# A two-layer decoder trunk: order of the FFN output products, and how stick-breaking q and k are stacked

## The chip, the cores and the metric

One core of one Trainium2 chip runs the whole kernel in one launch. The metric is the device time of one execution in microseconds (us), the median of several runs.

## The reference

The input is one sequence of 512 tokens with 1024 features. There are two layers; each is a mixer between two half-step SwiGLU feed-forward networks (FFNs), so there are four FFNs in all. Layer 0 mixes with a hybrid block (a gated recurrence beside attention with a forget gate), layer 1 with stick-breaking attention over 16 heads of 64 features.

```python
def _swiglu(h, w_in, w_out):
    a, b = jnp.split(h @ w_in, 2, axis=-1)
    return (jax.nn.silu(a) * b) @ w_out

# stick-breaking attention, one block of 128 queries
z = jnp.einsum('bhqd,bhkd->bhqk', qi, k) * scale
log_nb = jnp.where(mask, jax.nn.log_sigmoid(-z), 0.0)
after = lax.cumsum(log_nb, axis=3, reverse=True) - log_nb
w = jnp.where(mask, jnp.exp(jax.nn.log_sigmoid(z) + after), 0.0)
return jnp.einsum('bhqk,bhkd->bhqd', w, v)

for layer in range(2):
    x = x + 0.5 * _swiglu(_rmsnorm(x, g0), w_in0, w_out0)
    x = x + mixer(_rmsnorm(x, gm))
    x = x + 0.5 * _swiglu(_rmsnorm(x, g1), w_in1, w_out1)
```

The hidden width of an FFN is 2816, that is 22 tiles of 128.

## The kernel before

Everything is stored transposed, features on the 128 partitions and the 512 tokens along the row. Each fp32 operand is split into a rounded part `hi` (a cast on ScalarE, ACT) and the rest `lo` (a subtraction on VectorE, DVE), and each product is made of three matmuls on TensorE (PE): hi by hi, hi by lo, lo by hi. `split` (line 116) loads a weight and splits it, `parts` (line 443) splits one that is loaded or computed. The pool `wp` holds these weights for the whole kernel: three buffers `raw`, four `hi`, four `lo`.

In an FFN (`ffn`, line 330) the hidden tiles j run in five chunks: 0 to 3, 4 to 7, 8 to 11, 12 to 15, 16 to 21. The tiles of the first chunk are plain products of 512 columns (`plain`). From the second chunk on two hidden tiles at a time (`pair`, line 466) are computed by Strassen's scheme of seven products in place of eight. A product (`product`, line 450) is 24 matmuls of 256 columns with a weight of its own, w1, w2, w5, w6, w3, w7, w4 in the order in which they are used; the weights other than w1, w2 and w4 are sums that DVE makes (`add`, line 460). The products accumulate in three PSUM banks, `px` (w1, w6, w7, w4), `py` (w2) and `pz` (w5, w3), and ACT and DVE read them between (`keep`, `plus`, line 488), before the next product adds to the same bank. The seventh product, of w4, is `tail`: it is handed to the next pair, which calls it as `before()` behind its own w1 product, so that on PE the order is w1, w4 of the pair before, w2, w5, w6, w3, w7. In the last pair of an FFN the tail follows behind the pair. The operands (`ops`, made by `g_inputs`) are prepared during the first pair, step by step, with `next(operands)`.

`outputs(c, done)` (line 534) multiplies the hidden tiles of a finished chunk by the output weights: eight units, one for each 128 output features, each of 12 matmuls of 512 columns for a chunk of four, and of 18 for the last chunk of six. One split weight serves two units (in the last chunk one). A unit ends with the addition to x on DVE (line 549). Its PSUM bank is the tag `mm` (three banks, shared with `px`) or `po` (one). The outputs of chunk c-1 are made while chunk c is computed: `between(i)` (line 573) takes whole units behind certain products of the pair, by the table `OUTPUTS` (line 48). The outputs of the last chunk run at the end, one behind the other.

PE executes in the order of the code (`manual_schedule`). The instructions of the other engines and of the DMA queue are ordered by a planner at compile time, which takes the ready one that stands first in the code; the queue on SyncE (SP) and each engine then run in that order.

In stick-breaking attention (`stick`, line 1066) heads go in pairs p = 0 to 7, two heads (e, o) on the 128 partitions. `qk_tile(p)` projects q and k of a pair with 24 matmuls of 512 columns each; `evac` (line 1084) takes the result from PSUM. For each head a tile `qks` is built that holds 64 partitions of one half and 64 of another: for q the hi part and the lo part, for k the hi part twice. Besides, `kl` holds k's lo part with zeros in the other 64 partitions (two sets, for even and odd pairs). `score` (line 1124) takes them as operands of two matmuls (lines 1129 and 1130). Each block of scores then goes through ACT, GpSimd and DVE, is transposed (line 646), split into `tt` (lines 649 and 650) and multiplied by v (line 664). The other products of the stage fill PE between these steps (`Fill`, lines 188 to 218), weighed by an amount of work that must be done before each step. `stack` (line 292), four DMAs on SP, is used in the hybrid stage to build its own `qks`.

Of the kernel before, what the change touches and what calls it, by code (L numbers as in the profile page):

```python
# [1 line left out]

# [8 lines left out]
F32 = mybir.dt.float32  # L11
F32R = mybir.dt.float32r
# [34 lines left out]

OUTPUTS = [((0, 1, 2, 1, 1), (1, 0, 1, 0, 1)), ((0, 0, 2, 0, 2), (1, 0, 1, 0, 2)), ((0, 0, 2, 0, 2), (1, 0, 1, 0, 2)),
           ((0, 0, 1, 0, 1), (1, 0, 1, 0, 1), (1, 0, 0, 0, 1))]
# [19 lines left out]
def kernel(ctx: ExitStack, tc: tile.TileContext, x, par, ffn_in, ffn_in2, ffn_out, ffn_out2,  # L69
# [56 lines left out]
    def mm3(pt, pairs, start=True, stop=True):  # L126

        n = len(pairs)
        for i, ((ah, al), (bh, bl)) in enumerate(pairs):
            T.matmul(out=pt, lhsT=ah, rhs=bh, start=(start and i == 0), stop=False)  # L130
            T.matmul(out=pt, lhsT=ah, rhs=bl, start=False, stop=False)  # L131
            T.matmul(out=pt, lhsT=al, rhs=bh, start=False, stop=(stop and i == n - 1))  # L132

# [166 lines left out]
    def run(g):  # L300
        for _ in g:
            pass
# [27 lines left out]
    def ffn(f, g_next, last=False):  # L330
# [3 lines left out]
        with ExitStack() as es:  # L334
# [115 lines left out]
            def product(pt, w, o, start):  # L450
                h, l = ops[o]
                for c in range(2):
                    po = pt[:, 256 * c:256 * c + 256]
                    for k in range(4):
                        wh, wl = cols(w, 4 * c + k)
                        for q, (a, b) in enumerate(((wh, h), (wh, l), (wl, h))):
                            T.matmul(out=po, lhsT=a, rhs=b[:, k], start=start and c + k + q == 0,  # L457
                                     stop=k == 3 and q == 2, skip_group_check=not (start and c == 0))

# [6 lines left out]
            def pair(j, between, operands, before):  # L466
# [34 lines left out]
                between(0)  # L501
# [4 lines left out]
                between(1)  # L506
# [6 lines left out]
                between(2)  # L513
# [5 lines left out]
                between(3)  # L519
# [4 lines left out]
                between(4)  # L524
# [10 lines left out]
            def outputs(c, done):  # L535

                j0, j1 = CHUNKS[c]
                n = j1 - j0
                for d in range(KT):
                    if n > 4:  # L540
                        w = split(ffn_out2[f, d], n * P, "wo")
                    elif d % 2 == 0:
                        w2 = split(ffn_out[f, c, d // 2], D, "wo")
                    ws = [cols(w, k) if n > 4 else cols(w2, d % 2 * 4 + k) for k in range(n)]
                    tok = [slice(0, S)] if not (last and done) or d < KT - 1 else [slice(0, S // 2), slice(S // 2, S)]
                    for t in tok:
                        po = pmm() if (d + t.start) % 2 else psum("po", 1)
                        mm3(po[:, t], [(ws[k], tuple(q[:, t] for q in hid[j0 + k])) for k in range(n)])
                        V.scalar_tensor_tensor(out=xT[d][:, t], in0=po[:, t], scalar=0.5, in1=xT[d][:, t],  # L549
                                               op0=ALU.mult, op1=ALU.add)  # L550
                        if last and done:
                            SY.dma_start(out=out[d][:, t], in_=xT[d][:, t])
                    if done and not last:
                        prep(d, g_next)
                    yield
# [12 lines left out]
            def tail():  # L568
                pass

            for c in range(1, len(CHUNKS)):
                if f == 0 and c == 3:
                    channel_consts(gp.tile([P, S], F32, tag="p5", bufs=1, name="t4"))
                g = outputs(c - 1, False)
                for j, counts in zip(range(*CHUNKS[c], 2), OUTPUTS[c - 1]):
                    def between(i):
                        for _ in range(counts[i]):
                            next(g)

                    tail = pair(j, between, operands, tail)  # L580
                if c == len(CHUNKS) - 1:
                    tail()
                run(g)
# [482 lines left out]
    def stick(g_next):  # L1066
        with ExitStack() as es:
# [15 lines left out]
            def qk_tile(p):  # L1083
                def evac(j):
                    def go(pt):
# [6 lines left out]
                        halves = [slice(0, HD), slice(HD, P)]  # L1092
                        st = [mp.tile([P, S], F32R, tag=f"qk{j}{c}", bufs=2, name="qks") for c in "eo"]
                        if j == 0:

                            for t, a, b in zip(st, halves, halves[::-1]):
                                A.copy(out=t[a], in_=pt[a])
                                V.tensor_tensor(out=t[b], in0=pt[a], in1=t[a].bitcast(F32), op=ALU.subtract)
                            qk[p, j] = st
                        else:  # L1100
# [3 lines left out]
                            for t, l, a, b in zip(st, klo[p % 2], halves, halves[::-1]):  # L1104
                                A.copy(out=t[a], in_=kt[a])
                                V.tensor_tensor(out=l[a], in0=kt[a], in1=t[a].bitcast(F32), op=ALU.subtract)
                                A.copy(out=t[b], in_=kt[a])
                            qk[p, j] = st
# [144 lines left out]
```

## Time and profile before

| | us |
|---|---|
| median of three runs | 1869.08 |
| lowest and highest | 1867.19, 1870.18 |
| the profiled execution | 1865.11 |
| its span | 1863.4 |
| PE busy in the span | 1836.0 (99%) |
| DVE busy | 1413.3 (76%) |
| ACT busy | 955.3 (51%) |

The span is the stretch that the profile shows; the execution is 1.7 us longer. The granted clock of PE was 1.00 throughout. The first FFN takes about the first 345 us, the hybrid block goes to 575, the second and third FFN to 915 and 1258, stick-breaking to 1515, the last FFN to the end.

A timeline row gives start and duration in us, the engine, the line of the code, the operation and the tiles (out<-in, buffer numbers left out). The durations of matmuls overlap, so the pitch is read from start to start. PEld is PE's loading of weights, SPq the issuing of DMAs on SyncE. A row of `s<-`, `mm<-` or `t<-` with line 457 is a gate product; lines 130 to 132 with `wo` are output products.

### The profile page before, as it was taken

To read this page: it belongs to the slowest core of one execution; us is meant where nothing else is said; L and a number is where in the kernel's file an instruction comes from. 1 tells how busy PE (TensorE), PEld (TensorE's weight loads), DVE (VectorE), ACT (ScalarE), POOL (GpSimd) and SP (SyncE) were. 2 spreads that over 40 slices of the span, in tenths; PEclk is the share of its full clock that TensorE was granted. 3 is DMA by queue.
4 is the path that set the end of the run, shared out by engine and by line. 5 is a ranking of instruction groups with operands and counts; after the bars stand their busy time and mean duration, and the time that the engine had idled before them with its cause. 6 is when DMAs were issued, how large, how long until landed. Compare 5 with 4: busy or idle time off the path is not lost.

```text
span 1863.4 us, 29383 instructions
## 1 busy us (share of the span) xinstructions
PE 1836.0 (99%) x11818; PEld 1664.1 (89%) x11818; DVE 1413.3 (76%) x1892; ACT 955.3 (51%) x1399; POOL 122.2 (7%) x266
## 2 busy tenths in 40 slices
PE   8999999998999999999999999999999999999999
PEld 6899999898888899999889999988888888999997
DVE  8867776688878877676597777765889978777773
ACT  5444444467755444444454444445777654444441
POOL 2000000111100000000000000001333400000000
PEclk9999999999999999999999999999999999999999
DMA  5332332353233333332323333232212123333322
GB/s 184 102 103 92 104 113 75 95 163 108 81 94 102 102 97 97 102 114 77 128 80 109 106 103 102 88 99 98 69 57 69 57 91 102 97 111 105 96 76 95
DMA packets 57304, 183.65 MB, mean 99 GB/s; under 512 B 8016, under 2 KB 9296, under 8 KB 57168
## 3 DMA queue, kind: packets, MB, share of 16 engines
q1 hardware_dynamic: 57168, 181.77, 30.6%
q8 instruction: 93, 1.52, 0.3%
q14 instruction: 43, 0.35, 0.1%
HBM read 172.31 MB, written 2.10 MB: 94 GB/s over the span
## 4 chain that ended last, share of the span: by engine, by line
PE 88%; DVE 6%; ACT 2%; issue 2%; POOL 1%; DMA 0%; SPq 0%; POOLq 0%; DVEq 0%; ACTq 0%
PE mm L457 22%; PE s L457 11%; PE mm L130 6%; PE mm L132 6%; PE mm L131 6%; PE t L457 5%; PE po L130 4%; PE po L132 4%; PE po L131 4%; PE mm L246 2%; PE mm L248 2%; PE mm L247 2%; PE mm L227 1%; PE mm L228 1%; PE mm L229 1%
## 5 line engine op out<-in xcount | busy, mean ns | idle before, releaser
L446 ACT CAST hi_w<-sum 128x1024 fp32r<-128x1024 f32 x144 | 150.8, 1050 | 191.9 <-PE s L457 52.1
L447 DVE TENSOR_TENSOR lo_w<-sum,hi_w 128x1024 fp32r<-128x1024 f32 x144 | 176.0, 1224 | 95.3 <-ACT hi_w L446 94.7
L122 ACT CAST hi_wo<-raw_wo 128x1024 fp32r<-128x1024 f32 (+1 forms) x96 | 94.1, 980 | 152.4 <-PE mm L131 64.2
L446 ACT CAST hi_w<-raw 128x1024 fp32r<-128x1024 f32 x72 | 75.8, 1052 | 129.9 <-PE s L457 70.7
L123 DVE TENSOR_TENSOR lo_wo<-raw_wo,hi_wo 128x1024 fp32r<-128x1024 f32 (+1 forms) x96 | 108.8, 1133 | 23.7 <-ACT hi_wo L122 23.7
L132 PE MATMUL po<-g,lo_wo 128*128 128x512 f32 x320 | 125.1, 391 | 1.3 <-DVE lo_wo L123 1.3
L130 PE MATMUL mm<-g,hi_wo 128*128 128x512 f32 (+1 forms) x324 | 125.8, 388 | 0.0
L130 PE MATMUL po<-g,hi_wo 128*128 128x512 f32 x320 | 125.6, 392 | 0.0
L132 PE MATMUL mm<-g,lo_wo 128*128 128x512 f32 (+1 forms) x324 | 125.5, 387 | 0.0
L131 PE MATMUL mm<-g,hi_wo 128*128 128x512 f32 (+1 forms) x324 | 125.5, 387 | 0.0
L131 PE MATMUL po<-g,hi_wo 128*128 128x512 f32 x320 | 125.2, 391 | 0.0
L122 ACT CAST hi_w<-raw_w 128x1024 fp32r<-128x1024 f32 (+2 forms) x75 | 77.9, 1040 | 85.3 <-PE mm L131 42.5
L123 DVE TENSOR_TENSOR lo_w<-raw_w,hi_w 128x1024 fp32r<-128x1024 f32 (+2 forms) x75 | 90.7, 1209 | 30.0 <-ACT hi_w L122 29.8
L549 DVE SCALAR_TENSOR_TENSOR x<-mm,x 128x512 f32<-128x512 f32 (+1 forms) x81 | 55.3, 683 | 49.8 <-PE mm L132 49.3
L246 PE MATMUL mm<-hi_w,xh 128*128 128x256 f32 (+1 forms) x312 | 90.8, 291 | 2.2 <-DVE q L897 2.2
L463 DVE TENSOR_TENSOR sum<-a,a 128x1024 f32<-128x1024 f32 x36 | 44.1, 1225 | 58.4 <-DMA a<-in_dram 58.4
L248 PE MATMUL mm<-hi_w,xl 128*128 128x256 f32 (+1 forms) x312 | 88.4, 283 | 0.0
L247 PE MATMUL mm<-lo_w,xh 128*128 128x256 f32 (+1 forms) x312 | 88.2, 283 | 0.0
L447 DVE TENSOR_TENSOR lo_w<-raw,hi_w 128x1024 fp32r<-128x1024 f32 x72 | 87.8, 1219 | 0.0
L549 DVE SCALAR_TENSOR_TENSOR x<-po,x 128x512 f32<-128x512 f32 x80 | 55.1, 689 | 39.5 <-PE po L132 39.5
L457 PE MATMUL s<-t4l,hi_w 128*128 128x256 f32 x288 | 81.6, 283 | 0.0
L457 PE MATMUL s<-t2l,hi_w 128*128 128x256 f32 x288 | 81.4, 283 | 0.0
(480 smaller groups left out, 6314.7 us busy)
## 6 DMA issues: line engine op xcount, KB each, us to landing
raw_w<-in_dram SPq DMA_DIRECT2D x72, 512.0 KB, 3.4
a<-in_dram SPq DMA_DIRECT2D x72, 512.0 KB, 3.5
raw<-in_dram SPq DMA_DIRECT2D x72, 512.0 KB, 3.5
raw_wo<-in_dram SPq DMA_DIRECT2D x64, 512.0 KB, 3.5
raw_wo<-in_dram SPq DMA_DIRECT2D x32, 384.0 KB, 3.0
raw_who<-in_dram SPq DMA_DIRECT2D x16, 512.0 KB, 3.3
qks<-hs SPq DMA_DIRECT2D x24, 128.0 KB, 2.5
x<-in_dram SPq DMA_DIRECT2D x8, 256.0 KB, 4.6
```

The lines of the kernel that those rows point to most:

```text
L122: A.copy(out=hi[:, :n], in_=raw[:, :n])
L123: V.tensor_tensor(out=lo[:, :n], in0=raw[:, :n], in1=hi[:, :n].bitcast(F32), op=ALU.subtract)
L130: T.matmul(out=pt, lhsT=ah, rhs=bh, start=(start and i == 0), stop=False)
L131: T.matmul(out=pt, lhsT=ah, rhs=bl, start=False, stop=False)
L132: T.matmul(out=pt, lhsT=al, rhs=bh, start=False, stop=(stop and i == n - 1))
L246: T.matmul(out=pt, lhsT=ah, rhs=bh, start=(k == 0), stop=False)
L247: T.matmul(out=pt, lhsT=ah, rhs=bl, start=False, stop=False)
L248: T.matmul(out=pt, lhsT=al, rhs=bh, start=False, stop=(k == KT - 1))
L446: A.copy(out=hi, in_=src)
L447: V.tensor_tensor(out=lo, in0=src, in1=hi.bitcast(F32), op=ALU.subtract)
L457: T.matmul(out=po, lhsT=a, rhs=b[:, k], start=start and c + k + q == 0, stop=k == 3 and q == 2, skip_group_check=not (start and c == 0))
L549: V.scalar_tensor_tensor(out=xT[d][:, t], in0=po[:, t], scalar=0.5, in1=xT[d][:, t], op0=ALU.mult, op1=ALU.add)
```

## The change

1. The table `OUTPUTS` and the calls of `between` go. A queue of output products is kept for the FFN, and `product` takes from it one 512-column matmul at a time, evenly among its 24 matmuls of 256 columns; `quota` says how many a product takes. The outputs of chunk c-1 begin three products later than chunk c does (`LAG`) and run over into the first products of the next chunk. 96 matmuls are spread over 14 products, in the last chunk 84 over 18; the last 12 run behind the last tail.
2. In stick-breaking, q and k are split over all 128 partitions, one cast and one subtraction each, and the stacked tiles are filled by DMA: four for q, four for k and two for k's lo part.

```diff
-OUTPUTS = [((0, 1, 2, 1, 1), (1, 0, 1, 0, 1)), ((0, 0, 2, 0, 2), (1, 0, 1, 0, 2)), ((0, 0, 2, 0, 2), (1, 0, 1, 0, 2)),
-           ((0, 0, 1, 0, 1), (1, 0, 1, 0, 1), (1, 0, 0, 0, 1))]
+LAG = 3
...
+    def mm3_each(pt, pairs, done):
+        n = len(pairs)
+        for i, ((ah, al), (bh, bl)) in enumerate(pairs):
+            for q, (a, b) in enumerate(((ah, bh), (ah, bl), (al, bh))):
+                T.matmul(out=pt, lhsT=a, rhs=b, start=i + q == 0, stop=i == n - 1 and q == 2)
+                if i == n - 1 and q == 2:
+                    done()
+                yield
...
             def product(pt, w, o, start):
                 h, l = ops[o]
+                more = quota.pop(0) if quota else 0
+                at = 0
...
+                            at += 1
+                            for _ in range(at * more // 24 - (at - 1) * more // 24):
+                                next(queue[0])
...
                     for t in tok:
                         po = pmm() if (d + t.start) % 2 else psum("po", 1)
-                        mm3(po[:, t], [(ws[k], tuple(q[:, t] for q in hid[j0 + k])) for k in range(n)])
...
+                        yield from mm3_each(po[:, t], [(ws[k], tuple(q[:, t] for q in hid[j0 + k]))
+                                                       for k in range(n)], landed)
                     if done and not last:
                         prep(d, g_next)
-                    yield
...
-                g = outputs(c - 1, False)
...
+                queue[0] = chain(queue[0], outputs(c - 1, False))
+                n = 7 * (CHUNKS[c][1] - CHUNKS[c][0]) // 2
+                end = n if c == len(CHUNKS) - 1 else n + LAG
+                total = 84 if c == len(CHUNKS) - 1 else 96
+                steps = end - LAG
+                each = [(i + 1) * total // steps - i * total // steps for i in range(steps)]
+                if not quota:
+                    quota.extend([0] * LAG)
+                quota.extend(each)
+                for j in range(*CHUNKS[c], 2):
+                    tail = pair(j, operands, tail)
+            tail()
+            run(queue[0])
             run(outputs(len(CHUNKS) - 1, True))
...
+                        h, l = (mp.tile([P, S], F32R, tag=f"qk{c}", bufs=2, name="hs") for c in "hl")
                         if j == 0:
-                            for t, a, b in zip(st, halves, halves[::-1]):
-                                A.copy(out=t[a], in_=pt[a])
-                                V.tensor_tensor(out=t[b], in0=pt[a], in1=t[a].bitcast(F32), op=ALU.subtract)
+                            A.copy(out=h, in_=pt)
+                            V.tensor_tensor(out=l, in0=pt, in1=h.bitcast(F32), op=ALU.subtract)
+                            stack(st, h, l)
                         else:
                             kt = wk("kt", 1)
                             V.tensor_tensor(out=kt, in0=pt, in1=rb, op=ALU.mult)
-                            for t, l, a, b in zip(st, klo[p % 2], halves, halves[::-1]):
-                                A.copy(out=t[a], in_=kt[a])
-                                V.tensor_tensor(out=l[a], in0=kt[a], in1=t[a].bitcast(F32), op=ALU.subtract)
-                                A.copy(out=t[b], in_=kt[a])
+                            A.copy(out=h, in_=kt)
+                            V.tensor_tensor(out=l, in0=kt, in1=h.bitcast(F32), op=ALU.subtract)
+                            stack(st, h, h)
+                            for t, a in zip(klo[p % 2], (slice(0, HD), slice(HD, P))):
+                                SY.dma_start(out=t[a].bitcast(F32), in_=l[a].bitcast(F32))
```

The removed `between(i)` stood behind each product of `pair`; the body of `landed`, passed to `mm3_each` as `done`, is the addition to x of line 549 and, in the last outputs, the store.

## Rows read from the trace of the kernel before

**Rows 1.** the page, part 1: busy us (share of the span) and instructions
```profile
PE 1836.0 (99%) x11818; PEld 1664.1 (89%) x11818; DVE 1413.3 (76%) x1892; ACT 955.3 (51%) x1399; POOL 122.2 (7%) x266
```

**Rows 2.** windows (PE, PEld, DVE, ACT, POOL busy): gate stretches, stick-breaking, a first pair
```profile
sum 824.91, PE 824.91 PEld 776.93 DVE 604.28 ACT 383.93 POOL 0.00; mean PE 206.23 PEld 194.23 DVE 151.07 ACT 95.98 POOL 0.00
...
1258.00:1515.00 257.00, 251.18 (x1498) 220.26 (x1497) 216.21 (x360) 175.66 (x336) 77.20 (x195) 1.00 0.21 71
...
941.00:985.00 44.00, 44.00 (x241) 38.19 (x241) 40.08 (x45) 21.32 (x25) 0.00 (x0) 1.00 0.29 96
```

**Rows 3.** timeline of PE (start us, us, engine line op); lines are left out
```profile
136.59 0.39 PE L130 MATMUL mm<-g,hi_wo 128*128 128x512 f32 x1
...
139.31 0.28 PE L457 MATMUL s<-t2h,hi_w 128*128 128x256 f32 x1
...
142.16 0.28 PE L457 MATMUL mm<-t6h,hi_w 128*128 128x256 f32 x1
```

**Rows 4.** timelines of PE and of its weight loads at a border
```profile
206.56 0.28 PE L457 MATMUL mm<-t6h,lo_w 128*128 128x256 f32 x1
206.68 0.40 PE L130 MATMUL po<-g,hi_wo 128*128 128x512 f32 x1
206.91 0.40 PE L131 MATMUL po<-g,hi_wo 128*128 128x512 f32 x1
...
206.68 0.19 PEld L131 LDWEIGHTS po<-g,hi_wo 128*128 128x128 f32 x1
```

**Rows 5.** timeline of ACT, gate stage; brackets hold idle time before and releaser
```profile
139.28 1.05 ACT L122 CAST hi_wo<-raw_wo 128x1024 fp32r<-128x1024 f32 x1 [3.83 <-PE mm L131]
142.25 1.05 ACT L446 CAST hi_w<-raw 128x1024 fp32r<-128x1024 f32 x1 [1.91 <-PE s L457]
```

**Rows 6.** timeline of the DMA issues on SP, same stretch
```profile
132.14 0.33 SPq L440 DMA_DIRECT2D raw<-in_dram  x1
```

**Rows 7.** timelines of DVE and PE, first pair of the first FFN
```profile
68.36 1.24 DVE L123 TENSOR_TENSOR lo_wo<-raw_wo,hi_wo 128x1024 fp32r<-128x1024 f32 x1
...
69.65 0.50 PE L132 MATMUL po<-g,lo_wo 128*128 128x512 f32 x1 [1.29 <-DVE lo_wo L123]
```

**Rows 8.** timelines of PE and DVE, last pair of the first FFN
```profile
319.15 0.40 PE L130 MATMUL po<-g,hi_wo 128*128 128x512 f32 x1
...
321.90 0.28 PE L457 MATMUL mm<-t3h,hi_w 128*128 128x256 f32 x1
...
319.34 0.69 DVE L488 TENSOR_TENSOR ab<-mm,keep 128x512 f32<-128x512 f32 x1 [0.53 <-PE mm L457]
```

**Rows 9.** groups by line, stick-breaking stage (count, busy us, mean ns, idle before)
```profile
L1098 DVE TENSOR_TENSOR qks<-mm,qks 64x512 fp32r<-64x512 f32 x16 | 11.0, 688 | 1.1 <-ACT qks L1097 0.6
L1105 ACT CAST qks<-kt 64x512 fp32r<-64x512 f32 x16 | 9.9, 618 | 1.3 <-DVE kt L1103 1.2
L1097 ACT CAST qks<-mm 64x512 fp32r<-64x512 f32 x16 | 9.3, 581 | 6.9 <-DVE qks L1098 6.9
```

**Rows 10.** waits, stick-breaking stage (us in total, times, longest us)
```profile
ACT qks L1097 <- DVE qks L1098: 6.9, 7, 1.6
PE po L664 <- DVE tt L650: 4.1, 4, 1.3
```

**Rows 11.** timeline of SP, hybrid stage; DMA issues (KB each, us to landing)
```profile
521.08 0.59 SPq L296 DMA_DIRECT2D qks<-hs  x1
...
qks<-hs SPq DMA_DIRECT2D x24, 128.0 KB, 2.5
```

**Rows 12.** timelines of DVE and PE, pair 6 of the heads
```profile
1437.89 0.67 DVE L1103 TENSOR_TENSOR kt<-mm,rb 128x512 f32<-128x512 f32 x1
...
1442.68 0.28 PE L1130 MATMUL s<-kl0e,qks 128*128 128x128 f32 x1
```

**Rows 13.** timeline of weight loads, stick-breaking stage
```profile
1451.07 0.19 PEld L1129 LDWEIGHTS s<-qks 128*128 128x128 f32 x1
1451.18 0.19 PEld L1130 LDWEIGHTS s<-kl0e,qks 128*128 128x128 f32 x1
```

More of the change, by code (lines that the diff above doesn't have):

```diff
@@ L1 @@
 from contextlib import ExitStack
+from itertools import chain
 import numpy as np
@@ L464, in add, with pair @@
                 return t
-            def pair(j, between, operands, before):
+            def pair(j, operands, before):
                 src = ffn_in2[f, (j - PLAIN) // 2]
@@ L500, in pair @@
                 product(py, w2, 1, True)
-                between(0)
                 s2 = add(s1, a11, ALU.subtract, s1)
@@ L505, in pair @@
                 product(pz, w5, 4, True)
-                between(1)
                 p5 = keep(pz, gp, "p5")
@@ L512, in pair @@
                 product(px, w6, 5, False)
-                between(2)
                 u2 = keep(px, state, "acc")
@@ L518, in pair @@
                 product(pz, w3, 2, False)
-                between(3)
                 plus(quarter(0, 1), pz, u2)
@@ L523, in pair @@
                 product(px, w7, 6, False)
-                between(4)
                 plus(quarter(1, 1), px, p5)
@@ L547, in outputs, with landed @@
                         po = pmm() if (d + t.start) % 2 else psum("po", 1)
-                        mm3(po[:, t], [(ws[k], tuple(q[:, t] for q in hid[j0 + k])) for k in range(n)])
[L549 to L552, printed above, removed]
+                        def landed(po=po, d=d, t=t):
+                            V.scalar_tensor_tensor(out=xT[d][:, t], in0=po[:, t], scalar=0.5, in1=xT[d][:, t],
+                                                   op0=ALU.mult, op1=ALU.add)
+                            if last and done:
+                                SY.dma_start(out=out[d][:, t], in_=xT[d][:, t])
+                        yield from mm3_each(po[:, t], [(ws[k], tuple(q[:, t] for q in hid[j0 + k]))
+                                                       for k in range(n)], landed)
                     if done and not last:
                         prep(d, g_next)
-                    yield
+            queue = [iter(())]
+            quota = []
             es.enter_context(tc.manual_schedule(engines={mybir.EngineType.PE}))
@@ L573, in ffn @@
                     channel_consts(gp.tile([P, S], F32, tag="p5", bufs=1, name="t4"))
-                g = outputs(c - 1, False)
[L575 to L583, printed above, removed]
+                queue[0] = chain(queue[0], outputs(c - 1, False))
[11 more added lines that the diff above has]
+            run(queue[0])
             run(outputs(len(CHUNKS) - 1, True))
@@ L1091, in go @@
                                                 op0=ALU.mult)
-                        halves = [slice(0, HD), slice(HD, P)]
                         st = [mp.tile([P, S], F32R, tag=f"qk{j}{c}", bufs=2, name="qks") for c in "eo"]
+                        h, l = (mp.tile([P, S], F32R, tag=f"qk{c}", bufs=2, name="hs") for c in "hl")
+                        qk[p, j] = st
                         if j == 0:
-                            for t, a, b in zip(st, halves, halves[::-1]):
-                                A.copy(out=t[a], in_=pt[a])
-                                V.tensor_tensor(out=t[b], in0=pt[a], in1=t[a].bitcast(F32), op=ALU.subtract)
-                            qk[p, j] = st
+                            A.copy(out=h, in_=pt)
+                            V.tensor_tensor(out=l, in0=pt, in1=h.bitcast(F32), op=ALU.subtract)
+                            stack(st, h, l)
                         else:
@@ L1103, in go @@
                             V.tensor_tensor(out=kt, in0=pt, in1=rb, op=ALU.mult)
-                            for t, l, a, b in zip(st, klo[p % 2], halves, halves[::-1]):
-                                A.copy(out=t[a], in_=kt[a])
-                                V.tensor_tensor(out=l[a], in0=kt[a], in1=t[a].bitcast(F32), op=ALU.subtract)
-                                A.copy(out=t[b], in_=kt[a])
-                            qk[p, j] = st
+                            A.copy(out=h, in_=kt)
[3 more added lines that the diff above has]
+                                SY.dma_start(out=t[a].bitcast(F32), in_=l[a].bitcast(F32))
                     return go
```

## The prediction

> **What bounds the kernel now.** I read the page first. TensorE (PE) is busy 1836.0 of 1863.4 us [rows 1], so time is won or lost only where PE waits or where its matmuls stand further apart or closer. The windows by stage come next [rows 2]: in one long stretch from the gate stage of each of the four FFNs, 824.91 us together, PE is busy all 824.91, DVE 604.28 (73%) and ACT 383.93 (47%). In the stick-breaking stage PE is busy 251.18 of 257.00 us. So the FFN part of the change can't gain by removing waits, since these stretches have none; it gains only if matmuls come closer together. The stick part has 5.8 us of waits to work on.
>
> Third, the timeline of PE gives the pitch, start to start. 24 products of 256 columns take from 139.31 to 142.16, 0.119 us each; 12 of 512 columns take from 136.59 to 139.31, 0.227 each, and the first ones behind a gate product 0.23 [rows 3, 4]. At the border the 512 starts 0.12 us after the 256, as another 256 would, and the next 512 another 0.23 later [rows 4]: the pitch is set by a product's own width, not by its neighbour's.
>
> Fourth, the timeline of ACT shows how weights get their room. `hi` and `lo` have four buffers each, and a conversion (cast into `hi` on ACT, subtraction into `lo` on DVE) starts when PE gives one back. The casts keep the order of the code: a raw gate weight was fetched at 132.14, yet at 139.28 the returned buffer went to the output weight `hi_wo`, which stands earlier in the code, and the gate weight waited for the next one, at 142.25 [rows 5, 6]. That `hi_wo` is first used two gate products later, and this lead is why PE does not wait for it now.
>
> **The change part by part.**
> (1) Spreading. No matmul is added or removed. Of the 1536 output products that ran in units of 12, 4 x (3 x 96 + 84) = 1488 now stand singly, 6 or 7 (4 or 5 in the last chunk) in a run of 24 gate products. By the border rows that is worth nothing: a single 512 may take the 0.227 of a unit's end or the 0.23 of its start, and the units of now hold both [rows 3, 4]. Bounds 1488 x -0.003 to 1488 x +0.002, so -4.5 to +3; I take 0, between them.
>
> (2) The room for output weights. Today an output weight holds its buffer for one or two units. Spread out, its 24 matmuls last 3.5 products, and the next output weight is due at once after it: one of the four buffers is always taken. `split` still stands right ahead of the first matmul that uses it. I followed the four buffers in the order of the code, as [rows 5] show it. In chunks 1 to 3 the switch from one output weight to the next falls in two places: in the middle of w1's product (after 4 of its 7 single products) and at the start of w6's, each once a pair. When w1's product starts, the four hold w1, w4 of the pair before, w2 (next in the code) and the old output weight, so the new one must wait for the old one's buffer. `hi` of the old one is free after its 23rd matmul; from there to the first matmul with the new one lie 7 gate products and one output product, 7 x 0.119 + 0.23 = 1.06 us. The cast starts 0.09 us after PE's release (142.16, 142.25) and takes 1.05 us [rows 3, 5]; PE starts 0.06 us after its operand (68.36 + 1.24 = 69.60, 69.65), and that matmul stays 0.10 us longer, 0.50 where others have 0.40 [rows 4, 7]. That makes 1.30 against 1.06, a stall of 0.24 us. `lo` takes 1.24 us more [rows 7], ready at about 2.5; the third matmul is due at 1.06 + 2 x (0.23 + 3.5 x 0.119) + 0.24 = 2.6, so nothing is added if DVE is free. With DVE at 73% and ACT at 47% a conversion often sits out part of another instruction of 0.6 to 1.2 us. Bounds 0.2 and 1.5 us a switch; I take 0.5, nearer to the free case, since the code's order puts these conversions ahead of most others. 6 such switches an FFN, 24 in all: +12 us (5 to 36).
> At the switches in w6's product the buffers of w2 and w5 come back first. The source of w3 needs w6's subtraction and a DVE addition, so the output weight probably takes w2's buffer two products ahead and nobody waits; if not, it costs as above. Bounds 0 and 24 x 0.5 = 12 us; I take 0. In the last chunk only the switch in w1 of the third pair is short of time: 0 to 1 us, four times; I take +2.
>
> (3) The last tail. `tail` adds w4's product into `px`, whose content DVE must have read by then (line 488). In all pairs but the last, w1's product of the next pair lies between. In the last pair a unit of 12 lies there now, 319.15 to 321.90, and DVE reads in it from 319.34 for 0.69 us [rows 8]. After the change only one single product of 0.23 us covers it: 0.19 + 0.69 + 0.06 + 0.10 - 0.23 = 0.8 us, up to 2 if DVE is behind another instruction. I take 0.9 x 4 = +3.6 (3 to 8).
>
> (4) The first pair of each FFN. DVE prepares the operands there and is busy 40.08 of 44 us [rows 2]. Today 5 units (60 matmuls, some 13.7 us) stand in that pair and give it time, afterwards 20 (4.6 us). Against that, a `lo_wo` for which PE waits 1.29 us now [rows 7] is due later, behind 12 gate products. In the order of the code I find w3 and w7 ready ahead of their products, with little to spare. Bounds -1.3 and +8; I take 0.
>
> (5) Stick-breaking. For q two ACT casts of 0.58 and two DVE subtractions of 0.69 on 64 partitions become one of each on 128; for k four casts of 0.62 become one, two subtractions one [rows 9]. Eight pairs: 8 x (0.58 + 3 x 0.62) = 19.5 us of ACT and 8 x 2 x 0.69 = 11 us of DVE go, off PE's path except where PE waits. There the view of waits shows PE waiting for DVE's `tt` (line 650) 4 times, 4.1 us together, and ACT's second q cast waiting for the first subtraction 7 times, 6.9 us [rows 10]. I take 3 of the 4.1 as gone (bounds 0 and the stage's 5.8 us of idle).
> Added: 4 DMAs for q and 6 for k, 80 in all, on SP. In the hybrid stage such a DMA holds SP 0.59 us and lands 2.5 us after its issue [rows 11]. Behind them on SP stand the loads of raw weights; 10 x 0.59 = 5.9 us in a pair of some 26 us leaves them room, and they have three buffers of lead: 0. But k itself comes later: multiplication 0.67, cast 0.62, four issues 2.4, landing of the fifth 2.5 make 6.2 us, and in pair 6 its first score stands 1442.68 - 1437.89 = 4.8 us behind the multiplication [rows 12]: +1.4 us there (with the first and the last pair, which are near the limit too, 0 to 5); I take 1. Net of (5): -2 (-6 to +5).
>
> Sum: 0 + 12 + 0 + 2 + 3.6 + 0 - 2 = +15.6 us. The profiled execution took 1865.11 us, 1.7 beyond its span; the median of the three runs is 1869.08, 4.0 above it. The difference carries over: 1869.1 + 15.6 is about **1884.5 us**. 0.2% (3.7 us) is about what can be told from no change.
>
> **Rivals.**
> A. The output weights are converted early after all: the order on ACT is laid out anew, and they step ahead of w2, which has two products of time. Then (3) and (5) are left: 3.6 - 4 gives 1869, between 1864 and 1872. For it: gate weights have long leads. Against it: the casts keep the code's order where both sources are there [rows 5, 6].
> B. Weight loads were what spaces the 256-column products, and a single 512 gives them slack. In the gate stage a load starts with the matmul before its own [rows 4]; in the stick stage two loads follow each other after 0.11 us [rows 13]. If the 0.119 were the load's, one 256 for each 512 would fall to 0.11, 1488 x 0.008 = 12 us, and the 512s to 0.227, 4.5 us: 1869 - 16.5 = 1853 without the waits of (2) and (3), 1868 with them. Against it: the 256 right ahead of a 512 keeps 0.12 and the 512 its 0.23 [rows 4].
> [...]
> C. Slower by far: at every switch, w1's and w6's, the new conversion stands behind one more instruction on ACT and on DVE, some 1.1 us. It decides if DVE is near full around w1's product, where both gates, s1, w5 and w2 fall. 48 x (0.24 + 1.1) = 64 us and (3): 1937. Against it: DVE idles a quarter of the gate stage [rows 2].
>
> **How the numbers follow.** Forecast 0.52 (its own range 1873 to 1905, from the bounds of (2) to (5)), A 0.20, B 0.14, C 0.14. The range 1857 to 1908 holds A, two thirds of B and little of C: together about 0.8. Faster by over 0.2% (below 1865.3): most of B, a third of A and a little for a larger gain in (5), 0.21. Within 0.2%: the rest of A and B and the low end of the forecast, 0.20. Slower: 0.59.
>
> **What the profile would show.** Right: in the gate stages PE is no longer busy throughout, and rows of PE's output products name ACT `hi_wo` or DVE `lo_wo` as releaser, about 6 times an FFN, 0.2 to 1.5 us each; casts of `hi_wo` start in the middle of w1's product; PE waits for line 488 once near the end of each FFN; 0.119 and 0.23 stay. In the stick stage the four waits for `tt` are fewer, and PE waits before the first score of pair 6. Wrong: no such waits (A), or 256-column products beside a 512 at 0.11 (B).

## The result and the profile after

The changed kernel takes 1924.15 us (median of four runs, 1918.78 to 1925.38) against 1868.13 us for the kernel before: 1.0299 times as long, 95% interval 1.0284 to 1.0314, so 56 us slower (the median before is now of four runs, the three of the table in front and one more). The prediction was 1884.5 us with a range of 1857 to 1908. The profiled execution took 1918.78 us, 53.7 more than that of before (1865.11).

The page of the changed kernel, part 1, answers to [rows 1]. PE has the same number of instructions and is busy longer; DVE and ACT have 16 and 32 instructions less.

```profile
PE 1869.5 (98%) x11818; PEld 1676.3 (87%) x11818; DVE 1397.6 (73%) x1876; ACT 935.0 (49%) x1367; POOL 121.1 (6%) x266
```

Windows from the first to the last gate product of each FFN (us, then PE, PEld, DVE, ACT and POOL busy, the granted clock, DMA share, GB/s), first the sum line of the kernel before, then the four lines and the sum of the changed one:

```profile
sum 1056.98, PE 1055.69 PEld 993.39 DVE 777.89 ACT 483.43 POOL 0.00; mean PE 263.92 PEld 248.35 DVE 194.47 ACT 120.86 POOL 0.00
```
```profile
58.39:338.72 280.33, 272.46 (x1884) 251.29 (x1883) 197.13 (x230) 123.42 (x156) 0.00 (x0) 0.99 0.29 94
636.79:914.85 278.06, 272.62 (x1884) 251.32 (x1882) 191.33 (x209) 119.40 (x149) 0.00 (x0) 0.99 0.30 95
996.42:1273.71 277.29, 270.98 (x1884) 249.94 (x1882) 191.44 (x209) 119.35 (x149) 0.00 (x0) 1.00 0.30 95
1601.35:1877.74 276.39, 271.14 (x1883) 250.00 (x1882) 191.35 (x209) 119.43 (x149) 0.00 (x0) 1.00 0.30 95
sum 1112.07, PE 1087.21 PEld 1002.55 DVE 771.24 ACT 481.61 POOL 0.00; mean PE 271.80 PEld 250.64 DVE 192.81 ACT 120.40 POOL 0.00
```

All of the loss is here: 1112.1 - 1057.0 = 55.1 us. The stretch between the third and the fourth FFN's gate products, which holds stick-breaking, went from 330.1 to 327.6. PE's busy time shows only half of the loss (1112.07 - 1087.21 = 24.9 us not busy), because a matmul's recorded length (0.28 or 0.40 us) is more than its distance to the next (0.12 or 0.23), so a short wait is hidden under it, and matmuls at a slower pace count as busy as well. The starts tell more. I took the differences between starts of neighbouring matmuls in these stretches, called more than 15 ns over the usual 229 (512 columns) or 119 ns (256) a wait, and added these up by their place:

| place in the changed kernel | times | waits, us | predicted |
|---|---|---|---|
| w6's product of the first pair | 4 | 6.4 + 4.2 + 2.7 + 2.7 = 16.0 | 0 (-1.3 to +8) |
| w1's products | 24 | 22.2 | 12 (5 to 36) |
| w6's products of later pairs | 20 | 6.9 | 0 (0 to 12) |
| last chunk, w1's product of the third pair and others | 8 | 4.8 | 2 (0 to 4) |
| the last tail | 4 | 3.5 | 3.6 (3 to 8) |

The waits of PE and of its weight loads for output weights, and two of the stick stage (us in total, times, longest us), from the changed kernel:

```profile
PE po L138 <- ACT hi_wo L121: 12.0, 5, 3.8
PE po L138 <- DVE lo_wo L122: 3.3, 4, 0.8
PE mm L469 <- ACT hi_wo L121: 2.6, 4, 0.6
...
PE s L1150 <- DMA kl0e<-hs: 1.8, 1, 1.8
PE s L1150 <- DMA kl1e<-hs: 0.8, 1, 0.8
...
PEld po L138 <- ACT hi_wo L121: 25.2, 48, 4.0
PEld po L138 <- DVE lo_wo L122: 10.2, 27, 1.0
```

48 loads wait for `hi_wo` and 27 for `lo_wo`; before, PE's one wait for an output weight was that for `lo_wo` in [rows 7]. The four of `mm` on line 469 for `hi_wo` are misnamed: they are the last tails, whose gate product needs no output weight; what it waits for is DVE's line 503 (line 488 before).

**The first pair.** Timelines of PE, ACT and DVE in the third FFN of the changed kernel (start us, us, engine, line, operation; in brackets the idle time before and what ended it):

```profile
1005.27 0.28 PE L469 MATMUL mm<-t5h,hi_w 128*128 128x256 f32 x1
1007.96 0.50 PE L138 MATMUL po<-g,hi_wo 128*128 128x512 f32 x1 [2.42 <-ACT hi_wo L121]
...
1005.12 0.59 ACT L499 COPY keep<-s 128x512 f32<-128x512 f32 x1 [3.21 <-PE s L469]
1005.92 1.04 ACT L455 CAST hi_w<-sum 128x1024 fp32r<-128x1024 f32 x1 [0.21 <-DVE sum L478]
1006.87 1.04 ACT L121 CAST hi_wo<-raw_wo 128x1024 fp32r<-128x1024 f32 x1
...
1004.67 1.22 DVE L478 TENSOR_TENSOR sum<-raw,sum 128x1024 f32<-128x1024 f32 x1
```

ACT idles 3.21 us, then keeps p5, casts w3 as soon as DVE has made its source s4 (1004.67 + 1.22 = 1005.89), and only then casts `hi_wo`. In the code `hi_wo` stands behind w3's `parts`, as its `split` is called inside w6's product. Its raw weight had landed at 986.70. PE, which now meets its first output matmul four matmuls into w6's product, waits from 1005.39 (1005.27 + 0.12) to 1007.96.

**What the wait does to the clock.** Windows of the changed kernel, second FFN, where PE waits in the same place:

```profile
640.00:645.70 5.70, 5.70 (x51) 5.70 (x49) 4.28 (x6) 2.17 (x4) 0.00 (x0) 1.00 0.27 92
645.70:648.40 2.70, 0.28 (x3) 0.08 (x2) 1.59 (x2) 2.49 (x4) 0.00 (x0) 1.00 0.42 109
648.40:650.00 1.60, 1.60 (x8) 1.46 (x9) 1.60 (x3) 0.84 (x1) 0.00 (x0) 0.67 0.36 143
650.00:652.00 2.00, 2.00 (x10) 1.90 (x10) 0.87 (x1) 0.00 (x0) 0.00 (x0) 0.50 0.64 170
652.00:654.00 2.00, 2.00 (x15) 1.82 (x14) 0.00 (x0) 0.37 (x1) 0.00 (x0) 0.91 0.26 100
...
1008.00:1012.00 4.00, 4.00 (x28) 3.74 (x29) 2.50 (x3) 1.11 (x2) 0.00 (x0) 1.00 0.53 184
```

PE was busy throughout, then 0.28 of 2.70 us; after that the granted clock is at half, 0.50 from 648.95 to 652.37, and comes back to 1.00. That costs 1.5 us (4.2 in the table against 2.7), and as much in the first FFN, where it is 0.50 from 72.10 to 75.52, behind a wait of 4.0 us; behind the same wait of 2.6 us in the third (the last row) and fourth FFN the clock stayed at 1.00. The other three executions of the changed kernel have a mean granted clock of 0.993 to 0.995 where the profiled one has 0.997, and are 4.5 to 6.6 us longer. So the same wait of 2.6 us brings the loss in one FFN and not in two others, and the rows do not show why.

**The switches.** The second pair of a chunk, w1's product in the third FFN of the changed kernel (PE, ACT, DVE):

```profile
1055.40 0.39 PE L138 MATMUL mm<-g,lo_wo 128*128 128x512 f32 x1
...
1055.99 0.28 PE L469 MATMUL mm<-t0h,lo_w 128*128 128x256 f32 x1
1056.35 0.50 PE L138 MATMUL po<-g,hi_wo 128*128 128x512 f32 x1
1056.68 0.28 PE L469 MATMUL mm<-t0h,hi_w 128*128 128x256 f32 x1
...
1055.24 1.05 ACT L121 CAST hi_wo<-raw_wo 128x1024 fp32r<-128x1024 f32 x1 [0.87 <-PE mm L138]
...
1055.37 0.68 DVE L369 TENSOR_TENSOR g<-ab,g 128x512 fp32r<-128x512 f32 x1
1055.97 0.68 DVE L560 SCALAR_TENSOR_TENSOR x<-mm,x 128x512 f32<-128x512 f32 x1
1056.57 1.22 DVE L122 TENSOR_TENSOR lo_wo<-raw_wo,hi_wo 128x1024 fp32r<-128x1024 f32 x1
```

The cast starts when the old weight's `hi` comes back, and PE's matmul, due at 1055.99 + 0.12 = 1056.11, starts at 1056.35: 0.24 us late, as worked out in the prediction. It then holds PE 0.33 instead of 0.23. `lo_wo` stands behind the gate's subtraction and the addition of the unit just finished (line 560), ends at 1057.79, and costs the third matmul another 0.22 + 0.11. So a switch costs 0.67, where 0.5 was taken.

A switch in w6's product, the pair before (ACT; w2's product ends at 1034.90, w6's starts at 1039.36):

```profile
1035.01 1.05 ACT L455 CAST hi_w<-sum 128x1024 fp32r<-128x1024 f32 x1 [0.57 <-DVE sum L478]
...
1038.97 1.05 ACT L121 CAST hi_wo<-raw_wo 128x1024 fp32r<-128x1024 f32 x1 [2.90 <-PE mm L138]
```

The first is w3's cast, which runs as soon as w2's product is over. `hi_wo` waits 2.90 us for an output matmul (line 138), so it gets the old output weight's buffer here too, and PE stands 0.24 + 0.11 us at the switch.

### The profile page after: what moved, and what is told of

Same layout as the page of the kernel before. It is cut to its first block, busy times and chain, and to the rows that moved or that the text cites. A ratio compares the mean times of both kernels' runs of the same rounds, so it can differ in the third digit from the quotient of the medians.

```text
span 1917.1 us, 29573 instructions
## 1 busy us (share of the span) xinstructions
PE 1869.5 (98%) x11818; PEld 1676.3 (87%) x11818; DVE 1397.6 (73%) x1876; ACT 935.0 (49%) x1367; POOL 121.1 (6%) x266
## 5 line engine op out<-in xcount | busy, mean ns | idle before, releaser
L138 PE MATMUL mm<-g,hi_wo 128*128 128x512 f32 (+1 forms) x648 | 239.2, 391 | 0.0
L138 PEld LDWEIGHTS po<-g,hi_wo 128*128 128x128 f32 x640 | 120.7, 189 | 30.3 <-ACT hi_wo L121 25.2
L138 PE MATMUL po<-g,lo_wo 128*128 128x512 f32 x320 | 129.1, 404 | 4.7 <-DVE lo_wo L122 3.3
L138 PEld LDWEIGHTS mm<-g,hi_wo 128*128 128x128 f32 x648 | 121.6, 188 | 5.9
L560 DVE SCALAR_TENSOR_TENSOR x<-po,x 128x512 f32<-128x512 f32 x80 | 55.1, 689 | 90.5 <-PE po L138 90.5
L456 DVE TENSOR_TENSOR lo_w<-a,hi_w 128x1024 fp32r<-128x1024 f32 x36 | 44.1, 1225 | 68.6 <-ACT hi_w L455 68.6
L469 PE MATMUL mm<-t0h,lo_w 128*128 128x256 f32 x288 | 82.7, 287 | 1.8 <-DVE lo_w L456 1.7
L469 PE MATMUL mm<-t3h,hi_w 128*128 128x256 f32 x288 | 81.0, 281 | 2.6 <-ACT hi_wo L121 2.6
```

The source lines that it names most:

```text
L138: T.matmul(out=pt, lhsT=a, rhs=b, start=i + q == 0, stop=i == n - 1 and q == 2)
L456: V.tensor_tensor(out=lo, in0=src, in1=hi.bitcast(F32), op=ALU.subtract)
```

## The experiments

The kernel before took 1866.1 to 1866.6 us beside these runs; the ratios are to it. Stage times are from the starts in each profiled execution.

| run | us | ratio (95%) | gate stages, us | between FFN 3 and 4, us |
|---|---|---|---|---|
| kernel before | 1868.1 | 1 | 1057.0 | 330.1 |
| changed kernel | 1924.2 | 1.0299 (1.0284 to 1.0314) | 1112.1 | 327.6 |
| e1_stick_only | 1864.4 | 0.9985 (0.9976 to 0.9994) | 1057.3 | 326.8 |
| e2_ffn_only | 1927.1 | 1.0325 (1.0311 to 1.0339) | 1117.1 | 330.4 |
| e3_own_room | 1904.8 | 1.0198 (1.0181 to 1.0215) | 1098.0 | 327.1 |
| e4_early | 1878.9 | 1.0065 (1.0051 to 1.0079) | 1071.8 | 327.1 |
| e5_first_pair | 1906.9 | 1.0217 (1.0201 to 1.0232) | 1100.1 | 327.2 |
| e6_tail_cover | 1874.4 | 1.0041 (1.0028 to 1.0055) | 1068.6 | 326.7 |
| e7_threes | 1880.2 | 1.0072 (1.0058 to 1.0086) | 1071.8 | 327.6 |
| e8_by_head | 1861.4 | 0.9970 (0.9959 to 0.9982) | 1057.4 | 325.8 |
| e9_q_only | 1863.4 | 0.9989 (0.9981 to 0.9998) | 1057.2 | 327.2 |
| e10_twelves | 1872.1 | 1.0030 (1.0018 to 1.0042) | 1066.2 | 326.8 |

**One part at a time.** e1 has the FFN of before and the new `evac` of stick-breaking; e2 the new FFN and the old `evac`.

> The kernel before with the stick-breaking part of the change alone. Theory: the whole loss is in the FFN, and the stick stage gains what the trace of after shows between the gate stages of the third and the fourth FFN, 330.09 to 327.64 us: about 2.4 us below the kernel before (1864 to 1867). Rival: the gain of that stage came from the work that the spread FFN leaves at its borders, not from the stacking: then no difference, or slower by up to 3 us because PE waits before the first scores of pairs 6 and 7 (2.1 and 0.9 us in the trace of after). Each theory expects those two waits here as well.

> The changed kernel with the stick-breaking code of before: spreading alone. Theory: the two parts add up, so this is the changed kernel plus 2.4 us, about 1926 (58 us over the kernel before). Rival: the FFNs behind and ahead of the stick stage absorb part of it: below 1922.

2.0 us faster and 60.8 us slower: as the theory has it, the whole loss is the spreading and the stacking is a small gain. The two add up to 58.8, the changed kernel has 56.0; its lowest and highest run are 6.6 apart, so they are equal within what these runs tell. The waits before the first scores are in e1 too:

```profile
PE s L1130 <- DMA kl0e<-hs: 1.5, 1, 1.5
PE t L646 <- DVE be L1141: 0.6, 1, 0.6
PE po L664 <- DVE tt L650: 0.4, 2, 0.2
PE s L1130 <- DMA kl1e<-hs: 0.4, 1, 0.4
```

The waits of PE for `tt` fell from 4.1 us [rows 10] to 0.4, and ACT's wait for the first subtraction of q is no longer there.

**Room or order.** e3 gives every second output weight buffers of its own, e4 keeps four and changes only where the conversion stands in the code.

```diff
 # e3
-                        w2 = split(ffn_out[f, c, d // 2], D, "wo")
+                        w2 = split(ffn_out[f, c, d // 2], D, "wo", gp if d % 4 else None)   # own hi, lo in gp
```
```diff
 # e4; `early` is where outputs() looks before it splits, `sent` counts output matmuls
+            def ahead():
+                n = -(-sent[0] // 24)
+                if n < 16 and quota and 24 * n < sent[0] + quota[0]:
+                    early[n] = split(ffn_out[f, n // 4, n % 4], D, "wo")
...
                 w1 = parts(a11)
                 next(operands, 0)
+                ahead()
                 w2 = parts(a12)
...
+                ahead()
                 s4 = add(a12, s2, ALU.subtract, s2)
                 w3 = parts(s4)
```

> The changed kernel with hi and lo buffers of its own for every second output weight of chunks 0 to 3, so that a new output weight needn't wait until the old one returns its buffer. Theory room: the waits at the weight switches in w1's and w6's product (0.24 + 0.11 us for hi, 0.22 + 0.11 for lo, some 24 us together) vanish, the wait in the first pair of each FFN (2.6 us, 4.0 in the first FFN) stays because it stands behind the cast of w3 on ACT: 1898 to 1904, down from 1924. Rival order: the conversion is late because it stands late in the code, behind w2's and w3's, and its own buffer changes nothing: 1918 to 1926. Rival load: ACT and DVE have no time for it earlier and the waits move to the gate weights lo_w: 1912 to 1924.

> The changed kernel with four buffers as it has, but with the output weight that comes next split ahead of w2's parts in w1's product, and ahead of w3's in w6's, in the first pair too. Theory order: ACT takes the casts in the order of the code, so the output weight gets the buffer returned earlier and w2 or w3, which have one to two products of time, wait instead without anybody waiting for them: the switches' 24 us and the 2.6 to 4.0 us in the first pairs go, with them the slow clock behind these (granted 0.50 for 3.2 us in the second FFN): 1872 to 1888. Rival: with four buffers somebody must wait; the waits move to w2 and w3: 1900 to 1924. Rival for the first pair: DVE is the limit there (it has the next operands to make), so the wait only changes its name, and 10 us of the 40 stay.

e3 came 0.8 us above its range and e4 into the middle of its own. In e3 no output matmul waits at a switch any more, in w1's or in w6's product, so the room was what they waited for. Part of the gain went elsewhere: w1's products wait 15.8 us for `lo_w` where they waited 5.5, once 3.2 us with a slow clock behind it. The first pairs keep their wait (20.3 us with the slow clock, which follows in all four FFNs here; the mean granted clock of the profiled execution is 0.991). The view of waits of e3 also gives the last tail its right name:

```profile
PE po L141 <- ACT hi_wo L124: 10.7, 4, 3.5
PE mm L472 <- DVE lo_w L459: 8.5, 8, 3.1
...
PE mm L472 <- DVE ab L506: 2.2, 4, 0.5
```

e4 gets rid of both without a buffer more: the four buffers are handed out in the order of the code (in the first pair of its third FFN `hi_wo` is cast at 977.95, w3 at 983.10), and when the output weight stands ahead of w2 or w3, these get the later one and still have a product of time. Of the waits in the table above there remain 1.7 (first pair, first FFN alone), 7.9 (w1's products, for `lo_w`) and 3.5 us (tails). The rival "somebody must wait" is right for 2.4 us only, by which w1's waits for `lo_w` grew (5.5 to 7.9).

**The first pair alone.** e5 has `ahead()` only at the first output weight of each FFN.

> The changed kernel with only the first output weight of each FFN split ahead of s4 and w3; the other weights stay where they are. Theory: the wait in the first pair (2.6 us each, 4.0 in the first FFN) and the slow clock behind it are a cause of their own, 16 us in the profiled execution of after and up to 20 in its other executions: 1903 to 1908. The switches in w1's and w6's product keep their 0.24 + 0.11 us. Rival: the wait is DVE's, which is busy with the operands, and comes back as a wait for lo_w of w6 or w3: 1914 to 1922.

1906.9, in the theory's range: this one conversion in each FFN is 17 of the 56 us. Timeline of ACT and PE in the third FFN of e5:

```profile
992.70 1.05 ACT L455 CAST hi_w<-sum 128x1024 fp32r<-128x1024 f32 x1 [0.33 <-DVE sum L479]
993.65 1.05 ACT L121 CAST hi_wo<-raw_wo 128x1024 fp32r<-128x1024 f32 x1
...
997.62 0.28 PE L469 MATMUL mm<-t5h,hi_w 128*128 128x256 f32 x1
997.74 0.40 PE L138 MATMUL po<-g,hi_wo 128*128 128x512 f32 x1
...
998.80 1.05 ACT L455 CAST hi_w<-sum 128x1024 fp32r<-128x1024 f32 x1 [0.75 <-DVE sum L479]
```

`hi_wo` is ready at 994.70, 3 us ahead of PE's matmul, because its cast now stands ahead of w3's, the last row. The two timelines show what the place of a cast in ACT's order costs: 2.6 us of idle PE in the changed kernel, while ACT had 3.21 us free just before. DVE was not the limit: with the order changed, it keeps up but for 1.7 us in the first FFN. The granted clock of e5's profiled execution was 1.000. The rival came true for these 1.7 us alone: they are waits for `lo_w` of w6 and w3.

**The tail.** e6 is e4 with 12 output matmuls of the last chunk between w7's product and the last tail.

```diff
-                total = 84 if c == len(CHUNKS) - 1 else 96
-                steps = end - LAG
+                total = 72 if c == len(CHUNKS) - 1 else 96
+                steps = end - LAG - (c == len(CHUNKS) - 1)
...
+            for _ in range(12):
+                next(queue[0])
             tail()
```

> The kernel with the early splits, with 12 output matmuls of the last chunk taken from the spread and put between w7's product and the last tail, as before. Theory: the wait for line 503, 0.81 us in each FFN, goes: 3.2 us below the kernel with the early splits, about 1875.5 (1874 to 1877). Rival: the wait belongs to the end of the pair, where the gate and the addition stand behind each other on DVE, and comes back at the outputs behind the tail: 1878 to 1880.

4.5 us below e4, the stage 3.2 us shorter, and no wait at the tail. The theory holds.

**The distance of single matmuls.** Over the gate stages, waits left out, a 512-column matmul stood 229.0 ns from the next in the kernel before (1483 of them) and 232.4 in the changed one (1392); those of 256 columns 118.2 and 118.1. e7 is e4 with three output matmuls at a time, e10 is e6 with twelve at a time, taken as soon as one is due. In both, the condition in `ahead()` counts what is owed as well.

```diff
+                            owed[0] += at * more // 24 - (at - 1) * more // 24
+                            if owed[0] >= 3:            # e10: >= 1, and range(12)
+                                for _ in range(3):
+                                    next(queue[0])
```

> The kernel with the early splits, where output matmuls are taken three at a time (a product takes 6 or 9) in place of one by one. Theory: a 512-column matmul behind a 256-column one stands 232.4 ns from the next, one behind another 512 only 229.0; with two of three behind a 512 the mean is 230.1, 1488 x 2.3 ns = 3.4 us less: about 1875.5. Rival: the distance is that of two accumulations in turn, whatever the order, and stays at 232.4: 1878 to 1880. A second rival: the weight loads under the 256-column matmuls take their gain back (256 at 118.1 rises).

1880.2: missed. The first, second and third of a group stand 231.4, 231.9 and 231.6 ns from the next. So the neighbour doesn't set the distance, as I had thought. Sorted by their place in a unit, the kernel before tells what goes with it, though not why: the first seven output matmuls behind gate products have 228.6 to 233.4, the eighth to tenth 228.7 to 227.6, from the eleventh on, through a second unit that follows at once, 226.6 to 226.8. [rows 3] shows such a second unit (12 in 2.72 us), [rows 8] a first one (12 in 2.75). Groups of three never get that far. That the gap was 229.0 before comes from long runs.

> The kernel with the early splits and the covered tail, where output matmuls are taken twelve at a time as soon as one is due, so units as before, but at the places of the spread. Theory: the distance of 512-column matmuls falls only over the first ten behind gate products, from 231.6 to 226.7 ns, so threes can't gain and twelves give the mean of 229 back: 1488 x 3.4 ns = 5 us, and the old output weight no longer holds its buffer between units, so w1's lo_w waits (some 0.2 us each, 6 us together) go too: 1863 to 1870, against 1874.4 one by one. Rival: the distance is not what is left, the waits are those of the late start (LAG) and of the places: 1873 to 1876.

1872.1, between the two ranges: 2.3 us less than e6, where 5 and more were expected. The distance fell to 229.6, and the waits of w1's products for `lo_w` went from 7.4 to 0.1 us, but in the last chunk, whose weights are not split ahead, new ones of 1.7 to 3.7 us appeared, in w1's product of each FFN's last pair (8.9 us by the starts; the view counts idle time alone):

```profile
PE mm L469 <- DVE lo_w L456: 6.7, 5, 1.9
```

So part of what was left were the single matmuls and part the waits for w1's `lo_w`. The traces tell where these come from. DVE in the third FFN, first of the changed kernel, then of e10:

```profile
1049.62 1.22 DVE L478 TENSOR_TENSOR sum<-a,a 128x1024 f32<-128x1024 f32 x1 [0.34 <-DMA a<-in_dram]
1050.76 1.22 DVE L478 TENSOR_TENSOR sum<-raw,a 128x1024 f32<-128x1024 f32 x1
1051.89 1.22 DVE L456 TENSOR_TENSOR lo_w<-raw,hi_w 128x1024 fp32r<-128x1024 f32 x1
```
```profile
1019.60 1.23 DVE L456 TENSOR_TENSOR lo_w<-raw,hi_w 128x1024 fp32r<-128x1024 f32 x1 [0.21 <-ACT hi_w L455]
...
1021.69 1.22 DVE L482 TENSOR_TENSOR sum<-a,a 128x1024 f32<-128x1024 f32 x1 [0.27 <-DMA a<-in_dram]
```

In the changed kernel the sums s1 and s3 stand ahead of w1's `lo_w` on DVE in the 24 products of the table's second row, and s1 waits for the DMA of its raw weight; PE waits for `lo_w` in 15 of them. In the last two pairs of each FFN `lo_w` stands ahead of the sums, and PE never waits for it. e10 turns this round: `lo_w` is ahead in the 24 and behind the sums in each FFN's last pair, just where its new waits are. So the order on DVE makes these waits, and buffers of their own for output weights (e3) could not remove them. Why the planner puts the sums first is not shown, and no run changes this order alone.

**Stick-breaking.** e8 is e1 with k's DMAs ordered by head; e9 stacks q alone.

```diff
-                            stack(st, h, h)
-                            for t, a in zip(klo[p % 2], (slice(0, HD), slice(HD, P))):
-                                SY.dma_start(out=t[a].bitcast(F32), in_=l[a].bitcast(F32))
+                            for t, kl, a, o in zip(st, klo[p % 2], (top, low), (low, top)):
+                                SY.dma_start(out=t[a].bitcast(F32), in_=h[a].bitcast(F32))
+                                SY.dma_start(out=t[o].bitcast(F32), in_=h[a].bitcast(F32))
+                                SY.dma_start(out=kl[a].bitcast(F32), in_=l[a].bitcast(F32))
```

> The kernel before with the stick-breaking part alone, the six DMAs of k ordered by head: both halves of head e's tile, then e's kl, then the same for o. Theory: the wait before the first scores of pairs 6 and 7 is one for the fifth DMA; as the third it starts 1.2 us earlier, and 1.5 + 0.4 us of waits fall to about 0.3: 1862.5 to 1864 against 1864.4 for the same part with the kl last. Rival: the wait moves to head o's kl, which stays the sixth: no difference, 1864 to 1865.

1861.4, below the theory's range, and the fastest kernel of this study: 0.30% below the kernel before. Waits of PE in its stick stage:

```profile
PE s L1132 <- DVE be L1143: 1.0, 1, 1.0
PE t L646 <- DVE be L1143: 0.6, 1, 0.6
PE po L664 <- DVE tt L650: 0.4, 2, 0.2
```

No score waits for a `kl` any more (1.9 us in e1), but one waits 1.0 us for DVE's `be`, and the stage is 1.0 us shorter than in e1. The rest of the 3.0 us between the medians is, as far as the executions show, not the order's work but the clock's. In the hybrid stretch, whose code is the same, PE's clock is at half in e1 from 448.40 to 451.82 and from 513.26 to 516.67, and never in e8: 298.3 us against 296.7, with a mean granted clock of 0.998 and 1.000 over the profiled executions. The fastest executions of the two, each with a mean granted clock of 1.000, took 1861.17 and 1860.30 us. So the theory's gain is there, about 1 us of it, and the excess is luck.

> The kernel before with the stacking of q alone; k is built by ACT and DVE as before, so only 32 of the 80 added DMAs are there and no score waits for kl. Theory: the stick stage gains from the ACT and DVE time of both, and k, with three casts and one subtraction less a pair, gives more than half: 1 to 2.5 us below the kernel before, less than the 5 us of q and k ordered by head. Rival: the gain is q's alone, since q's second cast waited for the first subtraction (6.9 us in the trace of before): 4 to 6 us below the kernel before.

2.8 us below the kernel before, just past the theory's 2.5 and far from the rival's 4, but the theory's reason falls: q alone brings 2.9 of the 4.3 us that the stage gains in e8, so q and not k has the larger share.

## Why the prediction was wrong

The direction was right, and for w1's switches and the last tail the place and the mechanism as well; the waits in the first pair and in w6's product were not seen, and the size was 54 us against 15.6. By the prediction's own terms, in the profiled execution:

- **(1) Single matmuls**: taken 0 (-4.5 to +3). With 229.0 to 232.4 it is 1488 x 3.4 ns = 5.1 us, less 0.6 for the 256-column ones: +4.5. The step that failed is "the units of now hold both": the rows that I set beside each other, 0.227 and 0.23, differ by the place in a long run and not by the border; [rows 3] was the second of two units, the best case.
- **(2) Switches**: w1's 12 against 22.2, within its bounds. The `hi` wait is 0.24 as worked out, the 0.10 behind it as well; missed were `lo_wo` (0.33), which DVE does behind two instructions of 0.68, and the waits for w1's own `lo_w`, 5.5 us in all, behind the sums s1 and s3 on DVE. w6's 0 against 6.9: the step "takes w2's buffer two products ahead" is wrong. w3 stands ahead of the output weight in the code, its cast runs at 1035.01, as soon as w2's product is over, and `hi_wo` must wait for the old output weight until 1038.97; [rows 5] had shown that the casts keep the code's order. Last chunk 2 against 4.8: `lo_wo` again.
- **(3) Last tail**: 3.6 against 3.5, right.
- **(4) First pair**: 0 (-1.3 to +8) against 16.0, of which 14.3 are new (the kernel before has 1.75 us of waits in its gate stages). This is the step that failed worst. I followed w3 and w7, which are in time, and took the first output weight to be one of those that only wait longer for PE. I did not ask where its cast stands on ACT: behind w3's, whose source DVE delivers just when PE wants the output weight. The reading of DVE was off too: the window of [rows 2], 941 to 985, is plain tiles up to 966.45, where DVE is busy throughout; in the first pair itself, 966.45 to 997.2, it is busy 23.7 of 30.75 us. And I gave no price to what a wait of that length does to the clock, though it cost 1.5 us in two of the four FFNs.
- **(5) Stick-breaking**: -2 against -2.4, right in kind and partly by luck in size. The waits for `tt` fell by 3.7 us where 3 was taken, those for `be` by 1.1 where nothing was, and the waits before the first scores of pairs 6 and 7 added 1.8 + 0.8 = 2.6 where 1 was taken.

Together 4.5 + 22.2 + 6.9 + 4.8 + 3.5 + 14.3 - 2.4 = 53.8, and the two profiled executions differ by 53.7. So close an agreement is chance: the terms of the gate stages make 56.2 where 55.1 was measured, and the hybrid stretch is 1.4 us longer, with the clock at half from 444.15 to 447.57, which no term holds. The median's 56.0 holds some more slow clock. (The prediction's last step, 1869.1 + 15.6, is 1884.7 and not 1884.5.)

Rival A fell: the conversions are not early, unless the code puts them ahead (e4). Rival B fell: 256-column matmuls beside a 512 keep 117.6 to 118.5 ns. If the load was what spaces the 256s, those beside a 512 would have come closer, to the 0.11 us between two loads in [rows 13], and the rows do not show that. Rival C named DVE around w1's product, which is what the rows show for `lo_wo`, but there one switch costs 0.67 and not 1.34, and one in w6's product 0.35: 24 and 20 of them are some 23 us, not C's 64. That the whole loss is nearer to C's than to the forecast is chance.

The range failed because every large error had one sign. Of the 38 us that the sum fell short, the first pair has 14.3, w1's switches 10.2, w6's 6.9, the single matmuls 4.5 and the last chunk 2.8. The first pair and w6's switches were set at zero where their bounds lay almost wholly above it; the first pair and the single matmuls came out beyond their upper bounds.

## What to carry to other kernels

Before work is spread more finely among an engine's instructions, follow each operand that it needs back to the queue that makes it: what stands ahead of it there in the code, which buffer it will get, and from when both are free; splitting the output weights a few lines earlier was worth 45 of the 56 us here. When an estimate's bounds lie on one side of the value taken, the value is a bet on the edge: take the middle, or find the row.

## What was not expected of the hardware

- The distance of 512-column matmuls falls with the length of their run: 231.6 ns for the first behind 256-column ones, 228.6 to 233.4 up to the seventh, 226.6 to 226.8 from the eleventh to the twenty-fourth. No run shows why. Three in a row gain next to nothing over one (231.6, 232.4).
- After a wait PE loses another 0.10 to 0.11 us at the next matmul (0.33 from start to start instead of 0.23), at each of the 24 switches in w1's products and the 20 in w6's.
- A wait of 2.6 us was followed by half the clock (0.50) for 3.4 us in the second FFN and by none in the third and fourth, where it stayed at 1.00. In e10's fourth FFN a wait of 2.1 us was (from 1799.77; the mean granted clock of that execution is 0.998).
